# Rotary embedding on one core: the first batch comes as one software load, and SyncE asks only for the two tables

## The chip, the cores and the metric

The kernel runs on one core of one Trainium2 chip. The metric is the device time of one execution in microseconds (us); lower is better. The kernel before takes 316.7 us, the median of three runs (316.68 to 316.78).

## The reference

The kernel applies rotary position embedding to `x` of shape (8, 2048, 16, 64): batch, sequence, heads, head dimension, all float32. Two tables `cos` and `sin` of shape (2048, 32) are shared by all batches and heads.

```python
x1 = x[..., :32]
x2 = x[..., 32:]
out1 = x1 * cos - x2 * sin
out2 = x1 * sin + x2 * cos
out  = concatenate([out1, out2], axis=-1)      # float32, same shape as x
```

One batch is 2048 x 16 x 64 float32 numbers, 8.39 MB. Eight batches are read and eight are written, 134.2 MB in all, and each number takes part in two products and one sum.

## The kernel before, in words

**Tiling.** A batch is one tile `xt`: its 2048 positions are laid over 128 partitions with `J = 16` positions ("rows" here) in each, so a partition holds 16 x 1024 numbers, 64 KB of float32 in main memory, contiguous. In the core the tile is float16, 32 KB per partition. The float32 numbers become float16 while they are loaded and float32 again while they are stored, by the transfer itself; such transfers are issued by POOL (`nc.gpsimd.dma_start`), and the profile lists them as the software queue q0. Transfers that SyncE (SP) issues do not change the type; the profile lists them as the hardware queue q1. Both queues are served by the same 16 DMA engines, and each engine carries 8 of the 128 partitions.

**Work on a tile.** `rotate` is three VectorE (DVE) operations: `v = swapped halves of x * sin_h` (L73), `x = x * cos_h` in place (L79), `x = x + v` in place (L81). `sin_h` (float16, with the sign of the first half turned) and `cos_h` are made by ScalarE (ACT) from the float32 tables `sin_f` and `cos_f` (L95 to L97).

**Buffers.** Five tiles (`NBUF = 5`) hold the batches in turn: batches 5, 6 and 7 go into the buffers of batches 0, 1 and 2, so their loads wait until the stores of those have landed.

**The opening.** SP issues three transfers: `sin_f` (L40), then `head`, which is the first two rows (`JA = 2`) of batch 0 as float32 (L41, 1.05 MB), then `cos_f` (L45). POOL issues at the same time the load of the other fourteen rows of batch 0 (L52, 7.34 MB in main memory), a tiny store of zeros called `opening` (L85), and the load of batch 1 (L52, 8.39 MB). ACT turns `sin_f` into `sin_h`, copies `head` into the first two rows of tile 0 as float16 (L91), and then turns `cos_f` into `cos_h` (L97). DVE rotates the first two rows; POOL then stores row 0 (`first`, L107) and issues the loads of batches 2, 3 and 4.

**The middle.** DVE rotates the remaining fourteen rows of batch 0 and then the batches one by one. POOL issues each store when its batch is rotated, and the loads of batches 5 to 7 when their buffers are free. POOL's instructions run in a fixed order, and an issue that waits holds up those behind it. `ring` only keeps the order of the first software transfers on POOL: load 0, opening, load 1, first, loads 2, 3 and 4.

**The end.** Batch 7 is stored in three parts: nine rows (`gate`, L141) and five rows (`rest`, L143) by POOL, and the last two rows by SP (`end`, L152), for which ACT turns them back into float32 in the tile `head` (L151). SP's store waits until `gate` has landed.

Of the kernel before, what the change touches and what calls it, by code (L numbers as in the profile page):

```python
# [1 line left out]

# [4 lines left out]


@with_exitstack  # L10
def kernel(
    ctx: ExitStack,
    tc: tile.TileContext,
    x: bass.AP,
    cos: bass.AP,
    sin: bass.AP,
    out: bass.AP,
):
    nc = tc.nc
    f16 = mybir.dt.float16  # L20
    f32 = mybir.dt.float32

    B, S, H, D = x.shape
    Dh = D // 2
    P = nc.NUM_PARTITIONS
    J = S // P
    NBUF = 5

    const_pool = ctx.enter_context(tc.tile_pool(name="rope_const", bufs=1))
    io_pool = ctx.enter_context(tc.tile_pool(name="rope_io", bufs=NBUF))  # L30
    tmp_pool = ctx.enter_context(tc.tile_pool(name="rope_tmp", bufs=1))

    JA = 2
    head = const_pool.tile([P, JA, H, D], f32)
    x0 = x[0].rearrange("(p j) h d -> p j (h d)", j=J)
    sin_f = const_pool.tile([P, J, Dh], f32)
    cos_f = const_pool.tile([P, J, Dh], f32)
    cos_h = const_pool.tile([P, J, Dh], f16)
    sin_h = const_pool.tile([P, J, D], f16)
    nc.sync.dma_start(out=sin_f, in_=sin.rearrange("(p j) d -> p j d", j=J))  # L40
    nc.sync.dma_start(  # L41
        out=head.rearrange("p j h d -> p (j h d)"),
        in_=x0[:, 0:JA, :].rearrange("p j f -> p (j f)"),
    )
    nc.sync.dma_start(out=cos_f, in_=cos.rearrange("(p j) d -> p j d", j=J))  # L45

    loads = []

    def load(b):
        xt = io_pool.tile([P, J, H, D], f16)  # L50
        j0 = JA if b == 0 else 0
        dma = nc.gpsimd.dma_start(  # L52
            out=xt[:, j0:J, :, :].rearrange("p j h d -> p (j h d)"),
            in_=x[b].rearrange("(p j) h d -> p j (h d)", j=J)[:, j0:J, :].rearrange("p j f -> p (j f)"),
        )
        loads.append(dma)
        return xt

    def store(b, xt, j0=0):
        return nc.gpsimd.dma_start(  # L60
            out=out[b].rearrange("(p j) h d -> p j (h d)", j=J)[:, j0:J, :].rearrange("p j f -> p (j f)"),
            in_=xt[:, j0:J, :, :].rearrange("p j h d -> p (j h d)"),
        )

    def rotate(xt, j0, j1):
        v = tmp_pool.tile([P, J, H, D], f16)
        n = j1 - j0
        js = slice(j0, j1)
        shape = [P, n, H, 2, Dh]
        sin_b = sin_h[:, js, :].rearrange("p j (e d) -> p j e d", e=2).unsqueeze(2).to_broadcast(shape)  # L70
        cos_b = cos_h[:, js, :].unsqueeze(2).to_broadcast([P, n, 2 * H, Dh])
        xe = xt[:, js, :, :].rearrange("p j h (e d) -> p j h e d", e=2)
        nc.vector.tensor_mul(  # L73
            out=v[:, js, :, :].rearrange("p j h (e d) -> p j h e d", e=2),
            in0=xe[:, :, :, ::-1, :],
            in1=sin_b,
        )
        xw = xt[:, js, :, :].rearrange("p j h (e d) -> p j (h e) d", d=Dh)
        nc.vector.tensor_mul(out=xw, in0=xw, in1=cos_b)  # L79
        xa = xt[:, js, :, :].rearrange("p j h d -> p (j h d)")  # L80
        nc.vector.tensor_add(out=xa, in0=xa, in1=v[:, js, :, :].rearrange("p j h d -> p (j h d)"))  # L81


    tiles = [load(0)]
    opening = nc.gpsimd.dma_start(  # L85
        out=out[0].rearrange("(p j) h d -> p j (h d)", j=J)[0:P, 0, 0:1],
        in_=nc.const_aps.tensor(0.0, [P, 1], f32),
        allow_slow_non_contiguous=True,
    )
    tiles.append(load(1))  # L90
    nc.scalar.copy(  # L91
        out=tiles[0][:, 0:JA, :, :].rearrange("p j h d -> p (j h d)"),
        in_=head.rearrange("p j h d -> p (j h d)"),
    )
    nc.scalar.copy(out=sin_h[:, :, Dh:D], in_=sin_f)  # L95
    nc.scalar.mul(out=sin_h[:, :, 0:Dh], in_=sin_f, mul=-1.0)  # L96
    nc.scalar.copy(out=cos_h, in_=cos_f)  # L97
    rotate(tiles[0], 0, JA)
    def part(b, j0, j1):
        return (  # L100
            out[b].rearrange("(p j) h d -> p j (h d)", j=J)[:, j0:j1, :].rearrange("p j f -> p (j f)"),
            tiles[b][:, j0:j1, :, :].rearrange("p j h d -> p (j h d)"),
        )

    def store_rows(b, j0, j1):
        dst, src = part(b, j0, j1)
        return nc.gpsimd.dma_start(out=dst, in_=src)  # L107

    first = store_rows(0, 0, 1)
    tc.add_manual_dep(  # L110
        first.ins,
        opening.ins.name,
        mybir.DependencyInfo(mybir.DependencyClass.Sync, mybir.DependencyReason.DATA),
        reason="the result replaces the zeros",
    )
    ring = [loads[0], opening, loads[1], first]
    for b in range(2, NBUF):
        tiles.append(load(b))
        ring.append(loads[b])
    for a, b in zip(ring[1:], ring[:-1]):  # L120
        tc.add_manual_dep(
            a.ins,
            b.ins.name,
            mybir.DependencyInfo(mybir.DependencyClass.NoSync, mybir.DependencyReason.DATA),
            reason="order of the ring",
        )
    for b in range(B):
        rotate(tiles[b], JA if b == 0 else 0, J)
        if b < B - 1:
            st = store(b, tiles[b], 1 if b == 0 else 0)  # L130
            if b == 0:
                tc.add_manual_dep(
                    st.ins,
                    first.ins.name,
                    mybir.DependencyInfo(mybir.DependencyClass.NoSync, mybir.DependencyReason.DATA),
                    reason="order of the ring",
                )
        if b + NBUF < B:
            tiles.append(load(b + NBUF))
    dst, src = part(B - 1, 0, 9)  # L140
    gate = nc.gpsimd.dma_start(out=dst, in_=src)  # L141
    dst, src = part(B - 1, 9, J - JA)
    rest = nc.gpsimd.dma_start(out=dst, in_=src)  # L143
    tc.add_manual_dep(
        rest.ins,
        gate.ins.name,
        mybir.DependencyInfo(mybir.DependencyClass.NoSync, mybir.DependencyReason.DATA),
        reason="order of the ring",
    )
    dst, src = part(B - 1, J - JA, J)  # L150
    nc.scalar.copy(out=head.rearrange("p j h d -> p (j h d)"), in_=src)  # L151
    end = nc.sync.dma_start(out=dst, in_=head.rearrange("p j h d -> p (j h d)"))  # L152
    tc.add_manual_dep(
        end.ins,
        gate.ins.name,
        mybir.DependencyInfo(mybir.DependencyClass.Sync, mybir.DependencyReason.DATA),
        reason="the last rows go out behind this part",
    )


# [1 line left out]
_INS = ['x', 'cos', 'sin']  # L162
_OUTS = [((8, 2048, 16, 64), 'float32')]


# [23 lines left out]
```

## Time and profile before

| What | Value | Where it stands |
|---|---|---|
| median of three runs | 316.7 us | times (316.68 to 316.78) |
| profiled execution, first to last instruction | 314.8 us | span on the page |
| DVE busy | 209.1 us (66%) | part 1 |
| ACT busy | 6.8 us | part 1 |
| POOL busy | 10.4 us | part 1 |
| software queue q0, share of 16 engines | 98.1% | part 3 |
| hardware queue q1, share of 16 engines | 2.2% | part 3 |
| read and written in main memory | 67.63 MB and 67.11 MB, 428 GB/s over the span | part 3 |
| DVE waits for a load | 29.8 us, in two places | part 5 |

The profile has no time of the profiled execution other than its span; the timed runs are 1.9 us longer than that span, for what lies ahead of the first and behind the last instruction.

How to read it: part 3 counts the bytes that a transfer writes, so a load that turns float32 into float16 counts half of what it reads. That is why part 2 shows about 200 GB/s where loads run and about 400 GB/s where stores run, at the same busy share. In tables of windows, a DMA packet's whole time and bytes are put where the packet starts, so in short windows the share can be above 1 or 0 while the engines are busy throughout; sixteen large packets that start together show as one peak. "Landing" of a transfer is the time from the start of its issue until all sixteen engines have signalled it.

### The profile page before, as it was taken

To read this page: it belongs to the slowest core of one execution; us is meant where nothing else is said; L and a number is where in the kernel's file an instruction comes from. 1 tells how busy PE (TensorE), PEld (TensorE's weight loads), DVE (VectorE), ACT (ScalarE), POOL (GpSimd) and SP (SyncE) were. 2 spreads that over 40 slices of the span, in tenths; PEclk is the share of its full clock that TensorE was granted. 3 is DMA by queue.
4 is the path that set the end of the run, shared out by engine and by line. 5 is a ranking of instruction groups with operands and counts; after the bars stand their busy time and mean duration, and the time that the engine had idled before them with its cause. 6 is when DMAs were issued, how large, how long until landed. Compare 5 with 4: busy or idle time off the path is not lost.

```text
span 314.8 us, 125 instructions
## 1 busy us (share of the span) xinstructions
DVE 209.1 (66%) x27; ACT 6.8 (2%) x6; POOL 10.4 (3%) x23
## 2 busy tenths in 40 slices
DVE  0108999999999999999679999980009993000000
ACT  3200000000000000000000000000000002000000
POOL 2002000000000000010000000200000001000000
DMA  9899999999999899999999999999999999999998
GB/s 283 187 262 200 200 266 200 200 262 204 200 200 325 375 500 400 400 333 266 200 200 212 387 400 400 475 458 266 200 300 433 400 400 525 408 400 400 433 427 339
DMA packets 3201, 101.71 MB, mean 323 GB/s; under 512 B 385, under 2 KB 385, under 8 KB 769
## 3 DMA queue, kind: packets, MB, share of 16 engines
q0 software_dynamic: 2624, 99.09, 98.1%
q1 hardware_dynamic: 576, 2.62, 2.2%
q14 instruction: 1, 0.00, 0.0%
HBM read 67.63 MB, written 67.11 MB: 428 GB/s over the span
## 4 chain that ended last, share of the span: by engine, by line
DVE 25%; another core or an unknown queue 20%; DMA 19%; issue 18%; ACT 1%; POOL 1%; SPq 0%; POOLq 0%; DVEq 0%; ACTq 0%
DMA xt<-in_x_dram 12%; DVE xt L81 8%; DVE xt L79 8%; DVE v L73 8%; DMA cos_f<-in_cos_dram 7%; ACT head L151 1%; POOL out_dram L60 0%; POOL xt L52 0%; ACT cos_h L97 0%; SPq L41 0%; SPq L40 0%; POOLq L52 0%; DVEq L73 0%; ACTq L151 0%
## 5 line engine op out<-in xcount | busy, mean ns | idle before, releaser
L73 DVE TENSOR_TENSOR v<-xt,sin_h 128x16384 f16<-128x16384 f16 (+2 forms) x9 | 69.7, 7744 | 40.0 <-DMA xt<-in_x_dram 29.8
L79 DVE TENSOR_TENSOR xt<-xt,cos_h 128x16384 f16<-128x16384 f16 (+2 forms) x9 | 69.7, 7744 | 13.4 <-ACT cos_h L97 13.1
L81 DVE TENSOR_TENSOR xt<-xt,v 128x16384 f16<-128x16384 f16 (+2 forms) x9 | 69.7, 7744 | 0.3
L52 POOL DMA_DIRECT2D xt<-in_x_dram x8 | 4.4, 557 | 120.2 <-DMA out_dram<-xt 119.4
L151 ACT CAST head<-xt 128x2048 f32<-128x2048 f16 x1 | 1.9, 1897 | 238.6 <-DVE xt L81 238.6
L60 POOL DMA_DIRECT2D out_dram<-xt x7 | 3.7, 535 | 58.6 <-DVE xt L81 58.6
L141 POOL DMA_DIRECT2D out_dram<-xt x1 | 0.5, 533 | 50.6 <-DVE xt L81 50.6
L91 ACT CAST xt<-head 128x2048 f16<-128x2048 f32 x1 | 1.9, 1897 | 3.4 <-DMA head<-in_x_dram 3.4
L107 POOL DMA_DIRECT2D out_dram<-xt x1 | 0.5, 531 | 24.1 <-DVE xt L81 24.1
L95 ACT ACT_TABLE_LOAD x1 | 1.3, 1283 | 0.7 <-PEq L173 0.7
L97 ACT CAST cos_h<-cos_f 128x512 f16<-128x512 f32 x1 | 0.6, 617 | 13.7 <-DMA cos_f<-in_cos_dram 13.7
L95 ACT CAST sin_h<-sin_f 128x512 f16<-128x512 f32 x1 | 0.6, 617 | 1.5 <-DMA sin_f<-in_sin_dram 1.5
L96 ACT ACTIVATE sin_h<-sin_f 128x512 f16<-128x512 f32 x1 | 0.6, 624 | 0.0
L85 POOL DMA_DIRECT2D out_dram<-const-float32-0.0 x1 | 0.5, 545 | 0.0
L143 POOL DMA_DIRECT2D out_dram<-xt x1 | 0.5, 533 | 0.0
L173 POOL MEMSET const-float32-0.0<- 128x1 f32 x1 | 0.1, 98 | 0.2 <-issue 0.2
L173 POOL MEMSET const-bfloat16-1.0<- 128x1 bf16 x1 | 0.1, 101 | 0.0
L173 POOL MEMSET const-float32-1.0<- 128x1 f32 x1 | 0.1, 98 | 0.0
L173 POOL MEMSET const-uint8-127<- 128x1 uint8 x1 | 0.1, 98 | 0.0
## 6 DMA issues: line engine op xcount, KB each, us to landing
xt<-in_x_dram POOLq DMA_DIRECT2D x7, 4096.0 KB, 38.3
out_dram<-xt POOLq DMA_DIRECT2D x1, 7680.0 KB, 70.6
out_dram<-xt POOLq DMA_DIRECT2D x1, 4608.0 KB, 42.4
xt<-in_x_dram POOLq DMA_DIRECT2D x1, 3584.0 KB, 22.2
out_dram<-xt POOLq DMA_DIRECT2D x1, 2560.0 KB, 47.9
head<-in_x_dram SPq DMA_DIRECT2D x1, 1024.0 KB, 6.9
out_dram<-head SPq DMA_DIRECT2D x1, 1024.0 KB, 8.4
out_dram<-xt POOLq DMA_DIRECT2D x1, 512.0 KB, 17.5
```

The lines of the kernel that those rows point to most:

```text
L52: dma = nc.gpsimd.dma_start(out=xt[:, j0:J, :, :].rearrange("p j h d -> p (j h d)"), in_=x[b].rearrange("(p j) h d -> p j (h d)", j=J)[:, ...
L60: return nc.gpsimd.dma_start(out=out[b].rearrange("(p j) h d -> p j (h d)", j=J)[:, j0:J, :].rearrange("p j f -> p (j f)"), in_=xt[:, j0:J ...
L73: nc.vector.tensor_mul(out=v[:, js, :, :].rearrange("p j h (e d) -> p j h e d", e=2), in0=xe[:, :, :, ::-1, :], in1=sin_b,)
L79: nc.vector.tensor_mul(out=xw, in0=xw, in1=cos_b)
L81: nc.vector.tensor_add(out=xa, in0=xa, in1=v[:, js, :, :].rearrange("p j h d -> p (j h d)"))
L85: opening = nc.gpsimd.dma_start(out=out[0].rearrange("(p j) h d -> p j (h d)", j=J)[0:P, 0, 0:1], in_=nc.const_aps.tensor(0.0, [P, 1], f32 ...
L91: nc.scalar.copy(out=tiles[0][:, 0:JA, :, :].rearrange("p j h d -> p (j h d)"), in_=head.rearrange("p j h d -> p (j h d)"),)
L95: nc.scalar.copy(out=sin_h[:, :, Dh:D], in_=sin_f)
L96: nc.scalar.mul(out=sin_h[:, :, 0:Dh], in_=sin_f, mul=-1.0)
L97: nc.scalar.copy(out=cos_h, in_=cos_f)
L107: return nc.gpsimd.dma_start(out=dst, in_=src)
L151: nc.scalar.copy(out=head.rearrange("p j h d -> p (j h d)"), in_=src)
```

## The change

SP no longer loads the two float32 rows of batch 0; it issues `sin_f` and `cos_f` only. POOL's first load takes all sixteen rows of batch 0 (8.39 MB instead of 7.34 MB), in the same form as every other load. ACT's copy of `head` into the tile is gone. The float32 tile stays for the last two rows of batch 7, under the name `tail`. Nothing else is changed: the first two rows are still rotated on their own, row 0 is still stored first, and the loads of batches 2 to 4 still stand behind that store.

```diff
-    head = const_pool.tile([P, JA, H, D], f32)
-    x0 = x[0].rearrange("(p j) h d -> p j (h d)", j=J)
+    tail = const_pool.tile([P, JA, H, D], f32)
...
     nc.sync.dma_start(out=sin_f, in_=sin.rearrange("(p j) d -> p j d", j=J))
-    nc.sync.dma_start(
-        out=head.rearrange("p j h d -> p (j h d)"),
-        in_=x0[:, 0:JA, :].rearrange("p j f -> p (j f)"),
-    )
     nc.sync.dma_start(out=cos_f, in_=cos.rearrange("(p j) d -> p j d", j=J))
...
         xt = io_pool.tile([P, J, H, D], f16)
-        j0 = JA if b == 0 else 0
         dma = nc.gpsimd.dma_start(
-            out=xt[:, j0:J, :, :].rearrange("p j h d -> p (j h d)"),
-            in_=x[b].rearrange("(p j) h d -> p j (h d)", j=J)[:, j0:J, :].rearrange("p j f -> p (j f)"),
+            out=xt.rearrange("p j h d -> p (j h d)"),
+            in_=x[b].rearrange("(p j) h d -> p j (h d)", j=J),
         )
...
-    nc.scalar.copy(
-        out=tiles[0][:, 0:JA, :, :].rearrange("p j h d -> p (j h d)"),
-        in_=head.rearrange("p j h d -> p (j h d)"),
-    )
     nc.scalar.copy(out=sin_h[:, :, Dh:D], in_=sin_f)
...
-    nc.scalar.copy(out=head.rearrange("p j h d -> p (j h d)"), in_=src)
-    end = nc.sync.dma_start(out=dst, in_=head.rearrange("p j h d -> p (j h d)"))
+    nc.scalar.copy(out=tail.rearrange("p j h d -> p (j h d)"), in_=src)
+    end = nc.sync.dma_start(out=dst, in_=tail.rearrange("p j h d -> p (j h d)"))
```

## The prediction

> **What bounds the kernel now.** I read the shares of the DMA queues first, then the chain that ended last, then the order of instructions in the first 29 us, and last the tables of windows, wide ones over the span and narrow ones at both ends. The queues' shares:
>
> ```profile
> q0 software_dynamic: 2624, 99.09, 98.1%
> q1 hardware_dynamic: 576, 2.62, 2.2%
> ```
>
> Together they fill the 16 engines for the whole span. Wide windows say the same of each stretch (the columns are the window, its length, busy time and instructions of DVE, ACT and POOL, TensorE's clock, the DMA share, GB/s written):
>
> ```profile
> 42.50:102.20 59.70, 59.47 (x7) 0.00 (x0) 1.08 (x2) 1.00 1.04 234
> 120.70:140.10 19.40, 19.33 (x3) 0.00 (x0) 0.53 (x1) 1.00 1.01 405
> 236.60:305.30 68.70, 26.07 (x3) 1.90 (x1) 1.06 (x2) 1.00 1.00 425
> ```
>
> The share is 1.00 or more in all of them, while DVE does 26 us of work in the last 69. So the kernel is a stream of transfers without a hole: the end is where the stream starts, plus its bytes at the stream's pace, plus any hole. The pace: the store of batch 1 alone is in flight between two waits of the chain, at 120.74 and 140.05, so 8.39 MB of float32 take 19.31 us (434 GB/s), and two rows of a batch, an eighth, take 2.41 us.
>
> The chain gives the first 24 us to the wait for cos_f, which would make the change look like a gain:
>
> ```profile
> 1.63 22.05 DMA cos_f<-in_cos_dram
> 23.68 0.02 issue
> 23.70 0.63 ACT cos_h L97
> 24.33 0.02 issue
> 24.35 1.24 DVE xt L79
> ```
>
> But what this chain releases at 27.13, row 0's store and the loads of batches 2 to 4, goes into a queue in which the load of batch 1 is still running. The reader is to see that the chain follows instructions here, and the transfers are not short of work.
>
> The place that counts is where load 0's data begin. POOL issues it at 1.25 for 0.67 us; its first data come much later:
>
> ```profile
> 1.16 0.42 SPq L41 DMA_DIRECT2D head<-in_x_dram  x1
> 1.25 0.67 POOL L52 DMA_DIRECT2D xt<-in_x_dram  x1 [0.81 <-PEq L184]
> ...
> 2.80:5.20 2.40, 0.00 (x0) 1.15 (x2) 0.19 (x1) 1.00 1.07 443
> 5.20:5.40 0.20, 0.00 (x0) 0.00 (x0) 0.00 (x0) 1.00 3.05 737
> 5.40:5.60 0.20, 0.00 (x0) 0.00 (x0) 0.00 (x0) 1.00 8.09 1720
> 5.60:7.40 1.80, 0.00 (x0) 0.00 (x0) 0.00 (x0) 1.00 0.00 0
> 7.40:7.80 0.40, 0.00 (x0) 0.00 (x0) 0.00 (x0) 1.00 5.39 1147
> 9.60:10.00 0.40, 0.00 (x1) 0.36 (x1) 0.00 (x0) 1.00 5.55 1224
> ```
>
> A peak is sixteen large packets that start together, one per engine: 1147 GB/s for 0.4 us is 459 KB, a partition's fourteen rows in float16 (28,672 bytes) sixteen times. The peaks at 5.4, 7.6 and 9.8 are load 0's first three rounds. Until 5.4 the engines carried the tables and then head, at the full 443 GB/s. The question is whether load 0 could not begin before 5.4, or was ready and stood behind head.
>
> **The change part by part.** The sum is made against the profiled execution: its span is 314.8, and the page has no other time of it; the median of the runs shown, 316.7, is 1.9 above that span, and I carry this over.
>
> *Head's transfer goes:* 1.05 MB at the pace above, -2.41 us of stream (its own stretch, 2.95 to 5.4, is 2.45). *Load 0 gains the same two rows:* +2.41 us. The float32 bytes of the stream are as before, so these two cancel but for some 0.04.
>
> *cos_f is issued at about 1.16 instead of 1.63* and runs right behind sin_f. Before, its packets took turns with load 0's: the peak at 9.8 has 490 KB, 31 KB more than the one at 7.6. The rounds lie 2.2 us apart where 459 KB of float16, 0.92 MB of float32, need 2.11, so eight such turns cost some 0.7 us; alone, 0.26 MB at 434 GB/s is 0.6. Gain 0.1; I allow 0 to 0.3, since 2 KB packets may stream closer when alone.
>
> *A possible hole between the tables and load 0.* This is the only unknown of size. sin_f lands at 3.52 and its data end near 3.0 (head follows at full pace from 2.8 on); cos_f has the same size, so the tables end at about 3.5. Load 0 begins at the earliest when POOL is done with the issue, 1.92, and at the latest where it is seen, 5.4. So the hole is between 0 and 1.9 us. I take 0, from the row nearest in kind, a transfer of one queue that comes while the other has work, at the other end of the kernel:
>
> ```profile
> 305.55 0.35 SPq L152 DMA_DIRECT2D out_dram<-head  x1
> ...
> 308.00:310.70 2.70, 0.00 (x0) 0.00 (x0) 0.00 (x0) 1.00 0.95 394
> 310.70:313.60 2.90, 0.00 (x0) 0.00 (x0) 0.00 (x0) 1.00 0.88 362
> ```
>
> SP's store of the last two rows is issued at 305.55. For sin_f, from issue (0.74) to first data (the windows are empty until 1.7) it is about 1.0, so this store was ready near 306.6. Yet all of its 1.05 MB (362 GB/s for 2.9 us) start after 310.7, behind the five rows of `rest`, which were in the queue before it. Ready data waited 4.1 us; the engines had taken up the five or so packets ahead of it (0.75 us each: five of sixteen rows are 6.0 us, in eight rounds). So a transfer that is not moving need not be one that is not ready. At the start, head's eight packets per engine take 0.31 us each; if as many as five are taken up ahead, load 0 was there by about 4.0, and the hole is 0.5 at most.
>
> On this point the Trainium skill's page "DMA: Bandwidth & Descriptors" (Specifications) gives about 1 us to the first byte of a software transfer; load 0's 5.4 does not agree at face value, and by the page's figure the hole would be 0 and the sum -0.1, against +1.8 by the face value.
>
> *Load 0 lands whole.* It landed at 23.45 (1.25 + 22.2); now between 23.2 and 25.2, with the hole. The first L73 on two rows (1.23) used to run at 10.0, under the wait for cos_h; it now stands behind the load with L79 (1.22) and L81 (1.23). Row 0's store and loads 2 to 4, at 27.13 before, come at 23.2 to 25.2 + 3.7 + 0.3, so at 27.2 to 29.2. They are queued behind load 1, which ends some 19.3 us after load 0, at 42.5 or later. Slack 13 us, cost 0. `first` also waits for load 0's landing now, which its DVE operations have waited for already.
>
> *DVE runs up to 2 us later* through batches 0 to 4. It then waits 4.84 us for load 5 (before its L73 at 159.38), so the delay ends there. The stores it releases have far more room: the store of batch 0 is issued at 50.1 and landed at 120.7, behind loads 2 to 4. Cost 0; without that cover it would be the delay itself, up to 2 us.
>
> *ACT's copy L91* (1.90) goes; ACT is busy 2% of the span. *Issues:* SP loses one of 0.42, POOL has as many as before; no issue stands on the stream's path once it runs. *The end* (gate, rest, the two rows in `tail`) is untouched.
>
> Sum: 316.7 - 2.45 + 2.41 - 0.1 + 0 = 316.6.
>
> **The rivals.** *A hole at the start (slower).* If the queues take strict turns packet by packet, load 0 must have become ready only at 5.4, and head's 2.4 us were cover for it. Then the engines stand idle from 3.5 to 5.4, no later work makes up for it, as there is no other hole to shorten, and the time is 316.7 + 1.9 - 0.1 = 318.5 or a little less. It passes 0.2% when load 0's first data come after about 4.2. For it: the peaks at 9.8 and on show one packet of cos_f per engine in each round, which is a strict turn; and load 0 begins exactly where head ends. Against it: SP's store at the end took no turn for 4.1 us; and that load 0 became ready on sixteen engines just when each had finished head would be a coincidence of some tenths of a us.
> By the Trainium skill, same page (Queues, rings and completion order), an engine goes round-robin between queues packet by packet; the turns of cos_f agree with it, the end rows do not, and it is this rule that would give 318.5.
>
> *The head of the chain was a real limit (faster).* If the stream ran short before loads 2 to 4 arrive, an earlier cos_f would bring them earlier. The most it could give is what lay between load 0's landing and cos_f's use, 23.45 to 24.35, so 0.9 us and 315.8. Against it: the new order puts a third product (1.23) in the same place, and the share is 1.04 from 20 to 40 us.
>
> *The late DVE reaches the stream (slower).* It would need load 5's wait of 4.84 to be used up, so a delay over 4.8 where I have 2 at most: a delay of 6 would cost 1.2, 317.9.
>
> **How the numbers follow.** A difference of 0.2% (0.63 us) is about what a measurement of this kernel can tell from no change. The forecast, no hole or one under 0.7 us, has 0.69 and spans 316.2 (the tables streaming closer, pace differing by 0.05%) to 317.2. The hole has 0.23, between 317.3 and 318.5; I keep it that high because strict turns are plainly seen for cos_f. Late DVE 0.02. The faster rival has 0.06. So faster 0.06, same 0.69, slower 0.25. The forecast's range alone leaves out 3 in 10, so the range reaches to the end of the hole: 316.2 to 318.5.
>
> **What would show it.** In narrow windows of the changed kernel, the first peak of sixteen large packets (1311 GB/s over 0.4 us, 32,768 bytes each) stands near 3.5 if I am right, and at 5.4 behind empty windows if the hole is there; peaks then follow every 2.4 us with nothing between. cos_f lands before 7 instead of 23.7; the head of the chain no longer waits for it but for load 0. Row 0's store is issued at 27.2 to 29.2, DVE's wait for load 5 stays positive, and `gate` lands as far from the start of load 0 as before. Wrong would be an empty stretch between the tables and load 0, a share under 0.95 anywhere from 20 to 300, or a load longer than 19.3.

## The result, and the profile after

The changed kernel takes 318.57 us (median of 20 executions, 316.67 to 319.51) against 316.84 for the kernel before, measured beside it (20 executions). The ratio is 1.0039, 95% interval 1.0021 to 1.0057: slower by 0.4%, where I had forecast no change at 316.6. Two later measurements gave a ratio of 1.0026 (1.0004 to 1.0047) and 1.0036 (1.0014 to 1.0059).

The median hides what is new: the times have two heaps. Over all runs of this study, 27 of 45 executions of the changed kernel lie above 317.9 (up to 319.6; 17 of the first 20, then 4 of 12, none of 1 and 6 of 12) and the other 18 between 316.4 and 317.4, where the kernel before lies. Of the kernel before, 5 of 107 executions lie above 317.9. So most executions of the changed kernel lose 1.2 to 3 us, and the rest lose nothing.

The profiled execution took 318.2 with a span of 316.4, 1.6 above the span before. Its queues and the head of its chain:

```profile
q0 software_dynamic: 2624, 99.62, 98.6%
q1 hardware_dynamic: 432, 1.57, 1.3%
...
1.25 23.45 DMA xt<-in_x_dram
24.70 0.03 issue
24.72 0.02 DVEq L67
24.75 0.05 issue
24.80 1.24 DVE v L67
26.03 0.03 issue
```

The engines are as full as before over the span, and the chain now begins with load 0 and not with cos_f, as it should. Now the windows at load 0's start (columns as in the prediction):

```profile
2.80:3.20 0.40, 0.00 (x0) 0.00 (x0) 0.19 (x1) 1.00 1.23 364
3.20:3.60 0.40, 0.00 (x0) 0.40 (x1) 0.00 (x0) 1.00 5.59 1086
3.60:4.00 0.40, 0.00 (x0) 0.40 (x2) 0.00 (x0) 1.00 0.92 184
4.00:4.40 0.40, 0.00 (x0) 0.35 (x1) 0.00 (x0) 1.00 0.39 87
4.40:4.80 0.40, 0.00 (x0) 0.00 (x0) 0.00 (x0) 1.00 0.46 82
4.80:5.60 0.80, 0.00 (x0) 0.00 (x0) 0.00 (x0) 1.00 0.00 0
5.60:6.00 0.40, 0.00 (x0) 0.00 (x0) 0.00 (x0) 1.00 0.40 87
6.00:6.40 0.40, 0.00 (x0) 0.00 (x0) 0.00 (x0) 1.00 3.06 655
6.40:6.80 0.40, 0.00 (x0) 0.00 (x0) 0.00 (x0) 1.00 1.15 246
6.80:7.20 0.40, 0.00 (x0) 0.00 (x0) 0.00 (x0) 1.00 1.14 246
7.20:7.60 0.40, 0.00 (x0) 0.00 (x0) 0.00 (x0) 1.00 0.38 82
```

One packet of load 0 is 32,768 bytes written, 82 GB/s over a window of 0.4 us, so the last column counts packets. Load 0 begins behind the tables, at 3.2 to 3.6, and there is no hole until 5.4. But the sixteen engines do not begin together: twelve have started by 3.6 and four more start in 3.6 to 4.8, and the second round comes as 1, 8, 3, 3 and 1 packets over two us, where before each round was one peak of 0.4. The engines are apart by then, and they stay apart. The end of the kernel shows it, first before, then after:

```profile
310.80:313.20 2.40, 0.00 (x0) 0.00 (x0) 0.00 (x0) 1.00 1.00 413
313.20:313.60 0.40, 0.00 (x0) 0.00 (x0) 0.00 (x0) 1.00 0.21 82
313.60:314.00 0.40, 0.00 (x0) 0.00 (x0) 0.00 (x0) 1.00 0.00 0
```

```profile
313.60:314.00 0.40, 0.00 (x0) 0.00 (x0) 0.00 (x0) 1.00 0.35 143
314.00:314.40 0.40, 0.00 (x0) 0.00 (x0) 0.00 (x0) 1.00 0.10 41
314.40:314.80 0.40, 0.00 (x0) 0.00 (x0) 0.00 (x0) 1.00 0.05 20
314.80:315.20 0.40, 0.00 (x0) 0.00 (x0) 0.00 (x0) 1.00 0.05 20
```

The last rows go out in packets of 8 KB, 20 GB/s in such a window. Before, all engines end within 313.2 to 313.6. After, the share falls to 0.05, less than one of sixteen engines: from 314.4 on a single engine sends one packet per window while fifteen have nothing left. What was lost at 4 us is still missing at 315: in the records of single packets, the latest engine ends its first packet of load 0 1.6 us after the earliest (7.51 against 5.91), and at the end of the kernel the latest is 1.7 us behind the earliest (315.20 against 313.52).

### The profile page after: what moved, and what is told of

It reads as the page before. It is cut to its first block, busy times and chain, and to the rows that moved or that the text cites. A ratio compares the mean times of both kernels' runs of the same rounds, so it can differ in the third digit from the quotient of the medians.

```text
span 316.4 us, 121 instructions
## 1 busy us (share of the span) xinstructions
DVE 209.1 (66%) x27; ACT 4.9 (2%) x5; POOL 10.4 (3%) x23
## 4 chain that ended last, share of the span: by engine, by line
DVE 25%; another core or an unknown queue 20%; DMA 20%; issue 19%; POOL 1%; ACT 1%; DVEq 0%; POOLq 0%; PEldq 0%
DMA xt<-in_x_dram 20%; DVE v L67 8%; DVE xt L75 8%; DVE xt L73 8%; ACT tail L141 1%; POOL out_dram L54 0%; POOL xt L46 0%; DVEq L67 0%; POOLq L46 0%; DVEq L73 0%; PEldq L174 0%; POOLq L54 0%
## 5 line engine op out<-in xcount | busy, mean ns | idle before, releaser
L141 ACT CAST tail<-xt 128x2048 f32<-128x2048 f16 x1 | 1.9, 1898 | 239.9 <-DVE xt L75 239.9
```

The costliest lines, as they stand in the source:

```text
L141: nc.scalar.copy(out=tail.rearrange("p j h d -> p (j h d)"), in_=src)
```

## Experiments

The first group asks whether the loss lies in the lag of single engines, and whether head's 8 KB packets, the sixteen rows in one load, or the late first product matter. "Lag" is the time by which an engine falls behind the others in load 0's first round.

### The changed kernel again (three runs)

No edit.

> The changed kernel once more, for the spread of its runs and a second profile. In its first profile load 0 began at 3.2, as predicted, but not on all engines together: the first sixteen packets start over 1.35 us and take 2.43 to 3.50 us, and the DMA engines stay apart by 1.7 us to the end. Lag theory: the lag drawn in the first round differs from run to run, so the time moves between 316.6 (no lag) and 319.5, and the span of the profile exceeds 314.8 by as much as its last engine lags. Hole theory (all engines idle until 5.4): the time is the same in each run, 318.5, and the first round starts together.

> The changed kernel a third time, for a profile that may fall on an execution without lag (8 of its 12 last runs took 316.6 to 317.4, and 3 of the first 20). Lag theory: if its time is under 317.4, its first sixteen packets of load 0 start within 0.6 and the DMA engines end within 0.8 of each other; if it is above 318, one or more engines start load 0 late or slowly and end as much behind.

> The changed kernel beside the three others of this group on one chip, to compare how often executions carry a lag. Both remaining theories: a mixture, some at 316.5 to 317.4 and the rest at 318 to 319.6; at least a third of the executions slow.

Measured: 12 executions from 316.60 to 319.47, 4 of them above 318.7; one of 316.56; and 12 from 316.45 to 319.60, 6 of them above 318. The hole theory falls, as the time is not the same in each execution. The run of 316.56 has a span of 314.8, as before the change, and this start:

```profile
3.20:3.60 0.40, 0.00 (x0) 0.00 (x0) 0.00 (x0) 1.00 2.56 717
3.60:4.00 0.40, 0.00 (x0) 0.38 (x1) 0.00 (x0) 1.00 4.71 1034
4.00:4.40 0.40, 0.00 (x0) 0.40 (x2) 0.00 (x0) 1.00 0.00 0
4.40:4.80 0.40, 0.00 (x0) 0.40 (x2) 0.00 (x0) 1.00 0.00 0
4.80:5.60 0.80, 0.00 (x0) 0.47 (x1) 0.00 (x0) 1.00 0.00 0
5.60:6.00 0.40, 0.00 (x0) 0.00 (x0) 0.00 (x0) 1.00 1.15 246
6.00:6.40 0.40, 0.00 (x0) 0.00 (x0) 0.00 (x0) 1.00 4.94 1065
```

Both rounds lie within 0.8 us, 3 and 13 packets in the second. The same program with no lag is the 316.6 that I had forecast, to a tenth. The profile of 319.1 (span 317.3) still moves 20 GB/s on the mean of 315.6 to 316.8; these are three packets of 8 KB, from three engines. Span and lag go together.

The windows do not tell one engine from another, but the packed trace holds the start and length of every packet, and in a running stream an engine's next packet follows its last within 0.05 us, so the engines can be told apart. In the execution of 319.1 twelve engines end their first packet of load 0 by 6.31, one at 7.74 and three at 8.84 to 8.96; at the kernel's end twelve are through by 313.8, one at 314.98 and three at 316.10 to 316.11. The three start load 0 only at 5.83, 5.87 and 6.46, while the last table packet of any engine ends at 3.71: they stood idle for over 2 us. In the execution of 316.56 all sixteen end their first packet in 6.00 to 6.31 and their last in 313.2 to 313.6.

### Bulk data ahead of load 0, from another batch

```diff
     nc.sync.dma_start(out=sin_f, ...)
+    nc.sync.dma_start(out=tail, in_=x1[:, 0:JA, :])      # two rows of batch 1
     nc.sync.dma_start(out=cos_f, ...)
...
+        j0 = JA if b == 1 else 0                         # load 1 has 14 rows, load 0 all 16
...
+    nc.scalar.copy(out=tiles[1][:, 0:JA, :, :], in_=tail)
```

> Load 0 as in the changed kernel, sixteen rows in one software load; SyncE again carries 1.05 MB between the two tables, but it is two rows of batch 1, and load 1 has fourteen rows. Bytes as in both kernels. Lag theory (load 0 needs bulk data ahead of it on each engine): load 0's first peak is narrow again and the time is that of before, 316.7, with runs within 0.3. Size theory (the sixteen-row packets are what staggers): still 318 to 319. Late rows theory (DVE's first product now waits for the whole of load 0): still 318 to 319, since that stays as in the changed kernel.

Measured: 316.82 (316.48 to 317.82, 11 executions), ratio 1.000 (0.9986 to 1.0013). Load 0 is as in the changed kernel, and DVE's first product still waits for all of it; yet the loss is gone. So neither the sixteen rows nor the late rows cost anything that shows. What the change took away was the bulk transfer between the first table and load 0.

### Load 0 alone at the start (two runs)

```diff
+    nc.scalar.copy(out=tail, in_=zeros); nc.scalar.copy(out=sin_f, in_=tail[...]); nc.scalar.copy(out=cos_f, in_=tail[...])
     nc.sync.dma_start(out=sin_f, ...)
-    nc.sync.dma_start(out=cos_f, ...)
+    nc.scalar.dma_start(out=cos_f, ...)
```

> The changed kernel with both tables asked for only after about 5 us (three ScalarE copies of zeros stand ahead of them), one by SyncE and one by ScalarE, so that load 0 starts with nothing ahead of it. Lag theory: load 0 starts cold, its first sixteen packets spread as in the changed kernel or wider; the time is 318 to 320, as the tables' 1.2 us now lies in the stream behind an emptier start. Turns theory (the small table packets next to load 0's first ones are what staggers): the first peak is narrow, engines stay together, and only the emptier start costs, 1.2 or so: 317.9 with runs within 0.3. The first packet also shows when a software load without anything ahead of it starts: near 3 by the lag theory, 5.4 by the hole theory.

> The run with both tables later, once more, for more executions: 6 of 6 lay between 317.5 and 317.8. Overlap theory: again all within 0.4 of 317.7. Late descriptor theory: a third or more of the executions 1 to 2.5 us slower than the rest, as nothing hides a late start here either.

Measured: 317.70 (317.51 to 317.82, 6 executions), ratio 1.0030 (1.0018 to 1.0042); the second time 317.82 (317.50 to 318.01, 8 executions). No scatter in 14 executions. The windows of the first:

```profile
2.40:2.80 0.40, 0.00 (x0) 0.40 (x1) 0.40 (x2) 1.00 5.48 901
2.80:3.20 0.40, 0.00 (x0) 0.40 (x1) 0.18 (x1) 1.00 1.97 328
3.20:3.60 0.40, 0.00 (x0) 0.40 (x1) 0.00 (x0) 1.00 0.00 0
3.60:4.00 0.40, 0.00 (x0) 0.37 (x2) 0.00 (x0) 1.00 0.38 82
```

11, 4 and 1 packets: load 0, issued at 1.25, is there at 2.4 to 2.8 when nothing is ahead of it. This settles the term that I could only bound: load 0 was ready long before 5.4. The round is slow, (5.48 + 1.97 + 0.38) x 0.4 = 3.13 us per engine on the mean against 2.43, but the engines end it together, and the late one does not stay behind: it starts at 3.76 and takes 2.44, and all sixteen end in 5.65 to 6.25. My lag theory said that any start without bulk ahead draws lags; it falls. The turns theory's forecast, 317.9 with little scatter, is met. In these 14 executions a start from idle costs about 1 us, always the same, and draws no lag.

### One row of head instead of two

```diff
-        in_=x0[:, 0:JA, :]
+        in_=x0[:, 0:1, :]
...
-        j0 = JA if b == 0 else 0
+        j0 = 1 if b == 0 else 0
```

> The kernel before with one row of batch 0 by SyncE instead of two, and fifteen by the software load: the bulk ahead of load 0 ends near 4.2 instead of 5.4. Lag theory: 316.7 if 1.2 us of cover is enough for every engine's first packet, up to 317.5 if the slowest engine needs more. Hole theory (load 0 ready only at 5.4): a hole of 1.2 on all engines, 317.9, the same in each run.

Measured: 317.30 (316.91 to 317.67, 11 executions), ratio 1.0018 (1.0009 to 1.0026). No execution above 317.9, and not the 1.2 us of the hole theory. The median is 0.6 us longer, but not by a lag: in the profile of 317.08 all sixteen engines end within 0.5 us of each other, in 313.6 to 314.1 (before: 313.2 to 313.6). So half the cover was enough against lags here; where the loss comes from is not shown.

### Load 0 held until the tables have landed

```diff
+    tc.add_manual_dep(loads[0].ins, cos_dma.ins.name, DependencyInfo(Sync, DATA))
```

> The changed kernel with load 0's issue held until cos_f has landed, so that every engine is free when load 0 comes. Overlap theory (engines that still carry the last table packets when load 0 arrives on the others fall behind, as those others' 64 KB reads then go first): no engine lags, as in the run with late tables, but a hole of some 2 us (landing near 4, then 1.6 from issue to first data) and a slow first round of 0.7: 319.2, runs within 0.4. Cold start theory (any start of load 0 without bulk ahead draws lags at random): the same hole, and runs spread over 2 us as in the changed kernel: 319 to 321.5.

Measured: 319.86 (319.55 to 320.20, 4 executions), ratio 1.0098 (1.0084 to 1.0113), 0.7 above the forecast and with 0.65 of scatter. With the same tables ahead, but no longer on the engines when load 0 comes, the two heaps are gone in these four executions, at the price of the hole.

### Two software loads for batch 0

```diff
+        if b == 0:
+            nc.gpsimd.dma_start(out=xt[:, 0:JA], in_=x0[:, 0:JA])     # 8 KB packets first
```

> The changed kernel with batch 0 in two software loads, rows 0 and 1 (8 KB packets) and then rows 2 to 15. Nothing else differs. Overlap theory: a late engine waits behind 8 KB reads of the others, not 64 KB ones, so the lag is at most some 0.3 to 0.6 and the time 316.6 to 317.3 in every run. If instead the descriptors of load 0 themselves come late to some engines, the lag is as before and runs spread from 316.6 to 319.5.

Measured: 319.26 (316.77 to 319.62, 9 executions, 7 of them above 319), ratio 1.0064 (1.0044 to 1.0085). The idea that a late engine only waits behind the others' 64 KB reads falls: with 8 KB packets first, the lag is as large. In the packets of the execution of 319.27, twelve engines start load 0 in 3.43 to 3.76 and four only at 5.03 to 5.93; the twelve have their eight 8 KB packets done by 6.32, the four at 8.50 to 8.63, and at the kernel's end the four are through at 316.15 to 316.29 and the twelve by 313.99.

### Head behind both tables

```diff
     nc.sync.dma_start(out=sin_f, ...)
+    nc.sync.dma_start(out=cos_f, ...)
     nc.sync.dma_start(out=head, ...)
-    nc.sync.dma_start(out=cos_f, ...)
...                                          # on ScalarE, head's copy moves behind the work on the tables
```

> The kernel before with SyncE's order sin_f, cos_f, head instead of sin_f, head, cos_f. Lag theory: head's 8 KB packets still run on every engine when load 0 comes, so no lag: 316.5 to 316.8; cos_f lands near 4 instead of 23.7, and this gains nothing but its turns (0.1). If cos_f's late landing were worth anything, up to 0.9 less.

> The order sin_f, cos_f, head once more, for a profile of an execution above 318.5 (7 of 12 were). If a lagging engine only waits for load 0, it carries head's eight 8 KB packets (2.45 us) meanwhile and ends with the others, so a lag could not show in the time; if the engine stands still, its first load 0 packet or the one after starts late or takes long and head's packets come after it, and it ends 1 to 2.5 behind.

> As the run before it, for a second chance of a lagging execution.

Measured: 318.98 (316.69 to 319.48, 12 executions, 7 above 318.9), ratio 1.0046 (1.0026 to 1.0067); then 316.55, and 318.65. I had expected no lag. The kernel has head's transfer, and loses as the changed kernel does. The windows of the execution of 318.65:

```profile
3.60:4.00 0.40, 0.00 (x0) 0.40 (x1) 0.00 (x0) 1.00 2.16 466
4.00:4.40 0.40, 0.00 (x0) 0.40 (x2) 0.00 (x0) 1.00 0.00 0
4.40:4.80 0.40, 0.00 (x0) 0.40 (x2) 0.00 (x0) 1.00 0.46 72
4.80:5.60 0.80, 0.00 (x0) 0.42 (x1) 0.00 (x0) 1.00 0.41 72
5.60:6.00 0.40, 0.00 (x0) 0.00 (x0) 0.00 (x0) 1.00 2.04 492
```

Here a packet of load 0 is 28,672 bytes, 72 GB/s in 0.4 us. Load 0 follows the tables directly, before head, whose packets begin only from 5.6 on. One engine starts load 0 in 4.4 to 4.8 and two in 4.8 to 5.6 (72 GB/s for 0.8 us are two packets); nothing else starts between 4.0 and 5.6. By the packets, the three start load 0 at 4.57, 4.83 and 4.96, while the last table packet ends at 3.79, and their first packets take 2.64 to 2.92 us against 2.13 to 2.36 on the others. Head was issued at 1.64 to 2.06, so its packets should have been in the queue of these engines (the trace does not show when they arrive), and none of them moved: a lagging engine stands still, it does not do other work meanwhile. So head helps by its place ahead of load 0, not by its presence.

### cos_f later, without and with load 0 held

```diff
     nc.sync.dma_start(out=sin_f, ...)
-    nc.sync.dma_start(out=cos_f, ...)
+    nc.scalar.dma_start(out=cos_f, ...)      # behind two copies on ScalarE
...
+    tc.add_manual_dep(loads[0].ins, sin_dma.ins.name, DependencyInfo(Sync, DATA))     # the second run alone
```

> The changed kernel with only sin_f ahead of load 0; cos_f is asked for some 4 us later by ScalarE. sin_f's data end near 3.0, just before load 0 can begin. Overlap theory (the lag needs table packets still on the engines when load 0 arrives): seldom or no lag, runs within 0.5 at 316.8 to 317.5, a hole of up to 0.4 and a slow first round. Late descriptor theory (load 0 reaches some engines up to 2.5 us late at random, and only bulk data ahead hides it): slow executions as often as in the changed kernel of this group, up to 319.5.

> The run with cos_f later, which lagged in 7 of 10 executions, with load 0's issue also held until sin_f has landed (near 3.3). In that run load 0's first packets started at 2.65, while sin_f's last packets still ran. Overlap theory: no lag, all executions within 0.6 of each other, at 318.5 to 319.3 for the 2 us hole. Late descriptor theory: half of the executions 1 to 2.5 us slower than the fastest.

Measured without the hold: 318.89 (317.11 to 319.49, 10 executions, 7 above 318.6), ratio 1.0053 (1.0034 to 1.0071). I had expected few lags, since sin_f's data should have been through. They were not, because load 0 comes earlier than I had assumed: its first packets are in 2.4 to 2.8, and sin_f's still run.

```profile
2.40:2.80 0.40, 0.00 (x0) 0.40 (x1) 0.40 (x2) 1.00 1.91 517
2.80:3.20 0.40, 0.00 (x0) 0.40 (x1) 0.19 (x1) 1.00 4.39 799
3.20:3.60 0.40, 0.00 (x0) 0.40 (x1) 0.00 (x0) 1.00 1.40 246
```

With the hold: 319.67 (319.26 to 319.83, 4 executions), ratio 1.0095 (1.0078 to 1.0112); half a us above the forecast, and no two heaps. The pair's edits differ in the hold alone: with it, load 0's first packet starts at 5.04, two us after sin_f's last one, and without it while sin_f's packets still run.

### Tables by POOL, and tables by ScalarE with head first

```diff
-    nc.sync.dma_start(out=sin_f, ...)       # and cos_f
+    nc.gpsimd.dma_start(out=sin_f, ...)     # and cos_f, ahead of load 0 in the software queue; rest as in the changed kernel
```

> The changed kernel with both tables asked for by POOL ahead of load 0, in the same software queue, and nothing early on the hardware queue. Overlap theory, if it is about two queues on one engine: no lag, all executions within 0.5, some 1.0 to 1.5 above before for the later start of the stream: 317.7 to 318.2. If small packets ahead of load 0 are enough in any queue: a mixture, from 317.7 up to 320.

Measured: 320.12 (319.88 to 320.31, 4 executions), ratio 1.0107 (1.0092 to 1.0122): 2 us above the first forecast and at the top of the other, without scatter. Its end still trails off, at a share of 0.31 from 315.6 to 316.8, and in the packets of the execution of 319.96 load 0 starts over 2 us, from 4.40 to 6.45, while the last table packet ends at 4.63. Here the tables go as 128 packets of 4 KB. So one queue does not save it, nor do 4 KB packets as such, and an even time does not prove even engines.

```diff
-    nc.sync.dma_start(out=sin_f, ...)       # and cos_f
+    nc.scalar.dma_start(out=sin_f, ...)     # and cos_f; head by SyncE as in the kernel before
```

> The kernel before with head as SyncE's only early transfer and both tables asked for by ScalarE, so that head's 8 KB packets start at once and the tables take turns with them. Lag theory in either form: head still runs ahead of load 0, so few or no lagging executions: 316.3 to 316.8; if the engines fill sooner at the start than with sin_f's 2 KB packets first, up to 0.5 less than before. If small packets next to load 0's start are enough for a lag even under head: a mixture up to 319.

Measured: 316.79 (316.67 to 317.21, 11 executions), ratio 1.0001 (0.9993 to 1.0010). Equal to the kernel before; the earlier start of head gains nothing, and no execution lies above 317.9. No version here beats the kernel before.

### What the runs settle, and what stays open

Load 0 right behind or under the tables' 2 KB packets: two heaps in four kernels (the changed one, the two loads, head last, cos_f later; 49 of 78 executions above 317.9). Behind the tables in its own queue: four even executions, 3.5 us slower, with engines 2 us apart. Load 0 on idle engines: no two heaps in 22 executions of three kernels, and a fixed cost of 1 to 3 us. Load 0 behind one or two rows of a batch (4 KB or 8 KB packets of SyncE): none of 33 executions of three kernels above 317.9, and 5 of 107 in the kernel before, so the cover makes a lag rare and does not rule it out. The lag at load 0's start is the loss at the end: in the packets of 319.1, 318.65 and 319.27, three or four engines are 1.4 to 3 us late in the first round, and as many end 1.2 to 2.6 us after the others.

Why an engine stands still is not shown. The idea that it waits behind the others' 64 KB reads is contradicted by the two software loads. The idea that its share of load 0 comes late at random, whatever runs before, does not fit the idle starts, which draw no lag; that a share comes late only when table packets are on the engines is not excluded.

## Why the prediction was wrong

**The reading of the chain** was right: cos_f's wait had no worth. In the execution of 316.56 cos_f landed at 4.1 (1.15 + 3.0) instead of 23.7, and nothing was gained. In the profiled execution of 318.2 the sign "cos_f lands before 7" failed: it landed at 23.9, as one engine sent its last seven packets of cos_f one by one between its packets of load 0, from 5.90 to 21.14.

**Head against two more rows, the issues, ACT's copy:** right. The run with rows of batch 1 has the same load 0 and measures 1.000.

**The hole:** the value was right, 0 for the engines as a whole. Load 0's first data are seen at 3.2 to 3.6 behind the tables, and at 2.4 to 2.8 without them; the argument from the store at the end, that a waiting transfer need not be an unready one, held. The strict turns that the rival builds on do occur (in the execution of 318.65 every engine sends load 0's and head's packets in turn, from its first or second packet of load 0 on), but they do not mean that load 0 is ready only at 5.4. The rival comes near the measured median with 318.5 by luck, for its mechanism did not occur: no common idle stretch, and times from 316.4 to 319.6 in one program.

**Load 0 lands whole, DVE later:** right in what it costs. Row 0's store is issued at 28.90, inside 27.2 to 29.2, and DVE still waits 4.70 for load 5. That load 0 lands at 24.70, inside 23.2 to 25.2, is luck: this room was left for the hole, and a lag filled it. In the execution of 316.56 it lands at 23.5, in that of 319.1 at 26.2, outside.

**The step that failed is the first one,** "the end is where the stream starts, plus its bytes at the stream's pace, plus any hole". It treats sixteen engines as one. Each engine has its own part of each transfer, 8 of 128 partitions, and no other engine takes work from it; the end is that of the slowest. The sum had no term for engines that start unevenly, and I took the narrow peaks of the trace before as given, when it was head's transfer that made them narrow. The missing term is 0 to 3 us and differs from one execution to the next; in the profiled one it is the whole 1.6 of the span. In the sum I had given head the value of its bytes alone. That 18 of 45 executions lie at 316.4 to 317.4, around the forecast's 316.6, says that the other terms were of the right size.

By the Trainium skill, page "DMA: Bandwidth & Descriptors" (Specifications), a software transfer's first byte comes after about 1 us; the trace agrees within half a us where nothing is ahead: 1.15 to 1.55 from load 0's issue to its first packets.

## What to carry to other kernels

Where the transfers are the bound from end to end, what counts is the slowest of the sixteen engines, and a lag of the first microseconds was not made up in 310 us, as no engine takes another's share. So look at how wide the first rounds are, and at how the share falls off at the very end, not only at whether the stream has holes. Keep some bulk packets on every engine between small first transfers and the first large software load; and judge such a start by many executions, for the loss differs from one to the next.

## What was new about the hardware

- A DMA engine can stand still at the start of the first software load: three engines for 0.8 to 1.2 us in the execution of 318.65, with head's packets already issued behind, and three for 2.1 to 2.8 us in that of 319.1.
- The lag stays to the last packet: the kernel moves 20 GB/s, one engine's pace, from 314.4 to 315.2 of a span of 316.4.
- The first round of a software load from idle engines takes 3.13 us per engine on the mean instead of 2.43, and the engines end it within 0.6 us of each other.
